# State space stage of a hybrid decoder layer: the instructions of VectorE, ScalarE and TensorE in the order of the kernel's calls

## The chip, the cores and the metric

The kernel runs on one NeuronCore of a Trainium2 chip. The core has five engines that each work through a queue of their own: TensorE (PE in the profile) for matrix products and transposes, VectorE (DVE) and ScalarE (ACT) for element work, GpSimd (POOL) for more element work, and SyncE (SP), which here only issues DMA transfers. An instruction that needs another engine's result waits for a semaphore, and whatever stands behind it on its own engine waits with it. The metric is the device time of one call in microseconds (us), compared by the median of several runs.

## The reference

One layer of a decoder trunk on x of shape (1, 1024, 1024), all in float32. It has three sub-layers: parallel token mixing, cross-attention into 256 memory tokens, and a feed-forward block. The token mixing is a stick-breaking attention beside a Mamba-2 state space mixer (32 heads of 64 in 4 groups, state size 128, chunks of 128 positions), each gated and projected. The part that matters here is the mixer's chunked form. For each group and each chunk of 128 positions:

```
cb     = C . B^T                               (128 x 128, shared by the 8 heads of the group)
decay  = exp(a_cs[l] - a_cs[s]), s <= l        (per head)
y_diag = (cb * decay) . x                      (inside the chunk)
state  = state * exp(a_cs[last]) + B^T . (decay_to_end * x)
y_off  = C . state_before * exp(a_cs)          (from earlier chunks)
y      = (y_diag + y_off + d_skip * x) * silu(z)
y      = y * rsqrt(mean(y*y over the group) + eps) * g_norm
out   += y . w_br_ssm                          (the branch's projection)
```

## The kernel before

**Arithmetic.** Products that need float32 accuracy are made of three passes: each operand is split into a high part (a copy that is rounded, made by ScalarE, `hi_sb`, L119) and a low part (what the rounding lost, made by VectorE, `lo_of`, L122), and `mm3` (L124 to L128) sums high.high, high.low and low.high.

**Stages.** Input projection and convolution come first, then the attention, then the state space stage, then the attention's projection with the gates, the output projection, cross-attention and the feed-forward block. Each stage opens its own pools of buffers and closes them at its end.

**The state space stage** is a software pipeline over 32 steps n (4 groups g of 8 chunks c, `n = 8 g + c`), written as one loop (L1340 to L1361). One pass of the loop calls, in this order:

- `prep(n + 2)`: two matmuls into the banks `dec` (L1137) give the decay's exponents, ScalarE takes the exponentials (L1138), VectorE multiplies them with `cb` (L1139, tile `seg`, 128 x 1024). GpSimd weighs x for the state (L1144, `xw`), and ScalarE and VectorE split it (`s2r`, the high and low part). At each fourth chunk `open_four` loads and splits B and C and makes `cb` (L1114).
- parts of the memory projection for the later cross-attention (`mem_work`), spread over the first eight passes, and for some n the loading and splitting of the branch's weights (`branch_load`, L1236 and L1237).
- one `branch` (12 matmuls into a bank `mm`, and VectorE's addition into the sum `a`, L1250; for group 0 a copy by ScalarE, L1248).
- `states(n + 1)`: three matmuls into `pst`, GpSimd's decay of the state (L1161), VectorE's addition (L1162), then the split of the state into `sth` (ScalarE) and `stl` (VectorE).
- `outp(n)`: GpSimd's d_skip product (L1178), three matmuls into `po`, VectorE's scaling (L1183), GpSimd's addition (L1184), 32 small matmuls into `pd`, VectorE's addition of `pd` (L1194) and product with the gate `zs` (L1195), ScalarE's square with a sum (L1198, tile `junk`), GpSimd's reciprocal root in two instructions (L173 and L174, `rstd`), and ScalarE's scaling of y by it (L1200).
- a second `branch`.
- `flip(n - 2)`: four transposes into the bank `ptr`, whose high part ScalarE takes (L1216, `oth`) and whose low part VectorE takes (L1217, `otl`).

Two `branch` calls stand in each pass from n = 7 on; ten are left over when the loop ends and are called from the next stage, mixed with its loads of the attention's output (`m`, L1408).

**What sets the order.** The kernel is written against a scheduling layer. It takes the calls, simulates a schedule, and puts each engine's instructions into the order of that schedule; an instruction of a later call may so stand ahead of one of an earlier call where no data or buffer forbids it. Three engines are wrapped in a small class, `InTurn` (L34 to L51). While its flag `on` is set, each instruction that is issued through it gets an order edge, on the same engine and without a semaphore, behind the one issued through it before. Before the change the flag is set only around the openings of the cross-attention and feed-forward stages (`in_turn`, L1593, with `opening` and `lead_in`). GpSimd and SyncE are never wrapped.

**Buffers.** In PSUM (eight banks) `dec` and `mm` have two banks each, `pst`, `po`, `pd` and `ptr` one each. In SBUF the pool `t2` gives nine rooms to `xs`, `xw`, `zs`, `y` and `yo` (all shown as `s`), the pool `wr` three to raw weights and to the memory projection's results, and `seg` has three.

Of the kernel before, what the change touches and what calls it, by code (L numbers as in the profile page):

```python
# [54 lines left out]
def hybrid_block(ctx, tc, a, out, dbg=None):  # L55
    nc = tc.nc
    V, A, T = [InTurn(tc, e) for e in (nc.vector, nc.scalar, nc.tensor)]
# [12 lines left out]
    def mk(pl, shape, dt, tag, bufs=None):  # L70
        uid[0] += 1
        kw = {} if bufs is None else {"bufs": bufs}
        return pl.tile(shape, dt, tag=tag, name=f"{tag}_{uid[0]}", **kw)
# [50 lines left out]
    def mm3(ps, sh, sl, mh, ml, start, stop):  # L124
        first = T.matmul(ps, sh, mh, start=start, stop=False)  # L125
        T.matmul(ps, sh, ml, start=False, stop=False)  # L126
        T.matmul(ps, sl, mh, start=False, stop=stop)  # L127
        return first  # L128
# [874 lines left out]
    with ExitStack() as p3:  # L1003
# [112 lines left out]
        def prep(n):  # L1116

            g, c = divmod(n, NCH)
            q, ci = divmod(c, 4)
            if c == 0:  # L1120
                grp[g] = {}
            if ci == 0:
                open_four(g, q)
            f4 = four[g, q]
            cs = slice(ci * P, (ci + 1) * P)
            d = chk[n] = {}
            rows_ = slice(c * P, (c + 1) * P)
            cr = colrows[n % NROW]
            for j in range(2):
                nc.sync.dma_start(cr[ONES + j:ONES + j + 1].bitcast(F32), sum_d[j:j + 1, g * GH:(g + 1) * GH, rows_])  # L1130
            xs = d["xs"] = mk(t2, [P, HALF], F32, "s2")
            nc.sync.dma_start(xs, xs_d[g][rows_, :])
            seg = d["seg"] = mk(t4, [P, GH, P], F32, "s4")
            for j in range(2):
                hs = slice(4 * j, 4 * j + 4)
                pe = mk(ps, [P, 4, P], F32, "dec", bufs=2)
                T.matmul(pe, f4["keys"][:, cs], cr[:, hs, :], start=True, stop=True)  # L1137
                A.activation(seg[:, hs, :], pe, AF.Exp)  # L1138
            V.scalar_tensor_tensor(seg, seg, LARGE, f4["cb"][:, ci, :].unsqueeze(1).to_broadcast([P, GH, P]), ALU.min, ALU.mult)  # L1139
            d["ch"], d["cl"] = f4["ch"][:, cs], f4["cl"][:, cs]  # L1140
            if c < NCH - 1:
                d["bh"], d["bl"] = f4["bh"][:, ci, :], f4["bl"][:, ci, :]
                xw = mk(t2, [P, HALF], F32, "s2")
                G.tensor_tensor(v3(xw), v3(xs), bc(wm, c, g), ALU.mult)  # L1144
                xwh = d["xwh"] = mk(t2, [P, HALF], F32R, "s2r", bufs=4)
                xwl = d["xwl"] = mk(t2, [P, HALF], F32R, "s2r", bufs=4)
                hi_sb(xwh, xw, "a")
                lo_of(xwl, xw, xwh)

        def states(n):  # L1150
            g, c = divmod(n, NCH)
            d, gd = chk[n], grp[g]
            if c == NCH - 1:
                return
            pst_ = mk(ps, [P, HALF], F32, "pst")
            marks.append(mm3(pst_, d["bh"], d["bl"], d["xwh"], d["xwl"], True, True))
            state = mk(gb, [P, HALF], F32, "state")
            if c == 0:
                A.activation(state, pst_, AF.Copy)
            else:  # L1160
                G.tensor_tensor(v3(state), v3(gd["state"]), bc(cdm, c, g), ALU.mult)  # L1161
                V.tensor_tensor(state, state, pst_, ALU.add)  # L1162
            gd["state"] = state
            sth = mk(gb, [P, HALF], F32R, "sth")
            stl = mk(gb, [P, HALF], F32R, "stl")
            hi_sb(sth, state, "a")
            lo_of(stl, state, sth)
            gd["st", c + 1] = (sth, stl)

        def outp(n):  # L1170
            g, c = divmod(n, NCH)
            d, gd = chk[n], grp[g]
            rows_ = slice(c * P, (c + 1) * P)
            seg, xs = d["seg"], d["xs"]
            zs = mk(t2, [P, HALF], F32, "s2")
            nc.sync.dma_start(zs, zs_d[rows_, g * HALF:(g + 1) * HALF])
            y = mk(t2, [P, HALF], F32, "s2")
            G.tensor_tensor(v3(y), v3(xs), dsk[:, g * GH:(g + 1) * GH].unsqueeze(2).to_broadcast([P, GH, HD]), ALU.mult)  # L1178
            if c > 0:
                po = mk(ps, [P, HALF], F32, "po")  # L1180
                mm3(po, d["ch"], d["cl"], *gd["st", c], True, True)
                yo = mk(t2, [P, HALF], F32, "s2")
                V.tensor_tensor(v3(yo), v3(po), bc(eam, c, g), ALU.mult)  # L1183
                G.tensor_tensor(y, y, yo, ALU.add)  # L1184

            pd = mk(ps, [P, HALF], F32, "pd")
            for h in range(GH - 1, -1, -1):
                hs = slice(h * HD, (h + 1) * HD)
                for j in range(2):
                    r = slice(j * HD, (j + 1) * HD)  # L1190
                    ins = T.matmul(pd[r, hs], seg[:, h, r], xs[:, hs], start=True, stop=True)
                    if h == GH - 1 and j == 0:
                        marks.append(ins)
            V.tensor_tensor(y, y, pd, ALU.add)  # L1194
            V.tensor_tensor(y, y, zs, ALU.mult)  # L1195
            junk = mk(jk, [P, HALF], BF16, "junk")
            ms = mk(stats, [P, 1], F32, "ms")
            A.activation(junk, y, AF.Square, scale=float(HALF) ** -0.5, accum_out=ms)  # L1198

            A.activation(y, y, AF.Copy, scale=rstd_of(ms))  # L1200
            d["y"] = y
# [23 lines left out]
        def branch_load(g, fh, kk):  # L1225

            if (g, fh) not in brw:
                brw[g, fh] = halves()
            w = brw[g, fh]
            raw = mk(wr, [P, 2, HALF], F32, "wraw")  # L1230
            r0 = g * HALF + kk * 2 * P
            nc.sync.dma_start(raw, a["w_br_ssm"][0][r0:r0 + 2 * P, fh * HALF:(fh + 1) * HALF].rearrange("(k p) f -> p k f", p=P))
            for j in range(2):
                k = 2 * kk + j
                gain = pcol("g_ssm_norm", g * 4 + k)
                A.activation(w[:, k, 0], raw[:, j], AF.Copy, scale=gain)  # L1236
                V.scalar_tensor_tensor(w[:, k, 1], raw[:, j], gain, w[:, k, 0].bitcast(F32), ALU.mult, ALU.subtract)  # L1237

        def branch(g, half, f):
            oh, ol = grp[g]["oh", half], grp[g]["ol", half]  # L1240
            sl = slice(half * HALF, (half + 1) * HALF)
            w = brw[g, f // 4]
            fs = slice(f % 4 * P, (f % 4 + 1) * P)
            pb = mk(ps, [P, HALF], F32, "mm", bufs=2)
            for k in range(4):
                mm3(pb, w[:, k, 0, fs], w[:, k, 1, fs], oh[:, k, :], ol[:, k, :], k == 0, k == 3)
            if g == 0:
                A.activation(acc[f][:, sl], pb, AF.Copy)  # L1248
            else:
                V.tensor_tensor(acc[f][:, sl], acc[f][:, sl], pb, ALU.add)  # L1250
# [4 lines left out]
        def mem_quanta():  # L1255
# [63 lines left out]
            for i, ps_ in enumerate(parts):  # L1319
                if i + 2 < len(loads):  # L1320
                    yield loads[i + 2]
                yield from ps_

        for n in range(AHEAD):
            prep(n)
        mq = list(mem_quanta())
# [2 lines left out]
        def mem_work(upto):  # L1329
            while mq and NQ - len(mq) < upto:  # L1330
                mq.pop(0)()
# [8 lines left out]
        for n in range(-AHEAD, NN + 2):  # L1340
            if AHEAD <= n + AHEAD < NN:
                prep(n + AHEAD)
            mem_work((n + AHEAD) * NQ / MEM_SPAN)
            for l in loads.pop(n, []):
                branch_load(*l)
            if todo and todo[0][0] <= n:
                todo.pop(0)[1]()
            if 0 <= n + 1 < NN:
                states(n + 1)
            mem_work((n + AHEAD + 0.33) * NQ / MEM_SPAN)  # L1350
            if 0 <= n < NN:
                outp(n)
            mem_work((n + AHEAD + 0.67) * NQ / MEM_SPAN)
            if todo and todo[0][0] <= n:
                todo.pop(0)[1]()
            if 0 <= n - 2 < NN:
                flip(n - 2)
                if (n - 2) % 4 == 3:
                    g, c = divmod(n - 2, NCH)
                    fs = list(range(KT)) if c == 3 else list(range(4, KT)) + list(range(4))  # L1360
                    todo += [(n + 2, lambda g=g, hf_=c // 4, f=f: branch(g, hf_, f)) for f in fs]  # L1361

# [889 lines left out]
```

## Time and profile before

| | |
|---|---|
| runs of the kernel before | 2516.95, 2513.93, 2514.5 us (median 2514.5) |
| the profiled execution | 2516.72 us, of which the span of the trace is 2515.0 us |
| mean granted clock of TensorE | 0.995 |
| PE busy over the span | 2449.4 us (97%), 12306 matmuls |
| DVE busy | 1803.6 us (72%) |
| ACT busy | 1161.5 us (46%) |
| POOL busy | 720.2 us (29%) |
| first and last product with the gate (L1195) in the state space stage | 1105.7 and 1410.4 us |

All of the prediction's times are positions or durations in the profiled execution, in us from the start of its span. A row of the timeline gives start, duration, engine, line, operation, output and inputs, and in brackets how long the engine had been idle and what ended it. "PE" and its weight loads ("PEld") overlap, and neighbouring instructions of one engine overlap by about a tenth of a microsecond, so a sum of durations is a little longer than the time they take. A row with "x32: 671/676/689" gives count, shortest, median and longest duration in ns.

### The profile page before, as it was taken

The page shows a single profiled execution, that of the slowest core. Times are in us where ns is not written, and L with a number is a line of the kernel's source. Part 1 is how long each engine was busy: PE and PEld are TensorE (multiplying, and loading weights), DVE is VectorE, ACT ScalarE, POOL GpSimd, SP SyncE. Part 2 cuts the span into 40 slices and gives each one's busy share as a digit, 9 for nine tenths or more (in the row PEclk, how much of TensorE's full clock was granted, in tenths as well). Part 3 has the DMA queues.
Part 4 walks back from the last instruction along what each step waited for, and adds up shares of the span by engine and source line. Part 5 has one row for each costly group of instructions (what it writes and reads, how often), then busy time and mean ns, then how long its engine had stood idle before and what let it go on. Part 6 is the DMA issues. An engine that isn't in the chain of part 4 may idle for free. (4 is left out here: it accounts for less than half of the span.)

```text
span 2515.0 us, 33312 instructions
## 1 busy us (share of the span) xinstructions
PE 2449.4 (97%) x12306; PEld 2016.7 (80%) x12306; DVE 1803.6 (72%) x2205; ACT 1161.5 (46%) x2054; POOL 720.2 (29%) x581
## 2 busy tenths in 40 slices
PE   7999999999999999999999999999999999999998
PEld 5788888888877888877777787887888888888887
DVE  7665777767587878689888674577368665666997
ACT  5333455555555665566644312344335333344433
POOL 3221545443111111146666241104011332220001
PEclk9999999999999999999999999999999999999999
DMA  7431443333534343366333481322142322234322
GB/s 248 157 118 49 138 145 107 109 101 93 160 97 109 95 117 91 94 191 206 98 100 88 136 273 64 131 94 67 67 151 63 101 80 76 93 98 165 131 101 101
DMA packets 249132, 295.62 MB, mean 118 GB/s; under 512 B 17023, under 2 KB 169096, under 8 KB 248842
## 3 DMA queue, kind: packets, MB, share of 16 engines
q1 hardware_dynamic: 248682, 292.45, 36.9%
q8 instruction: 97, 1.59, 0.3%
q10 hardware_dynamic: 288, 1.05, 0.1%
q14 instruction: 65, 0.53, 0.1%
HBM read 202.20 MB, written 74.45 MB: 110 GB/s over the span
## 5 line engine op out<-in xcount | busy, mean ns | idle before, releaser
L911 DVE TENSOR_TENSOR_SCAN n<-n,mask 128x128 f32<-128x128 f32 (+7 forms) x128 | 189.8, 1510 | 23.7 <-ACT n L910 22.4
L122 DVE TENSOR_TENSOR sw<-sf,sw 128x512 fp32r<-128x512 f32 x142 | 129.5, 916 | 69.6 <-ACT sw L119 67.6
L119 ACT ACTIVATE sw<-sf 128x512 fp32r<-128x512 f32 x142 | 88.9, 628 | 155.8 <-PE mm L230 139.2
L928 ACT ACTIVATE wth<-tr,mone 128x512 fp32r<-128x512 f32 x192 | 110.7, 585 | 83.6 <-PE tr L925 81.7
L929 DVE SCALAR_TENSOR_TENSOR wtl<-tr,wth 128x512 fp32r<-128x512 f32 x192 | 99.7, 544 | 48.6 <-ACT wth L928 48.6
L693 DVE SCALAR_TENSOR_TENSOR b<-b,prmT,b 128x1023 f32<-128x1023 f32 (+2 forms) x72 | 109.7, 1523 | 16.9 <-ACT b L687 16.3
L196 POOL TENSOR_TENSOR sf<-wr,wr 128x512 f32<-128x512 f32 x36 | 51.8, 1438 | 232.7 <-DMA wr<-in_w_gu_dram 95.1
L122 DVE TENSOR_TENSOR sw<-wr,sw 128x512 fp32r<-128x512 f32 x107 | 100.3, 939 | 24.4 <-ACT sw L119 24.3
L229 PE MATMUL mm<-h,sw 128*128 128x512 f32 x288 | 112.0, 389 | 0.0
L230 PE MATMUL mm<-h,sw 128*128 128x512 f32 x288 | 111.7, 389 | 0.0
L228 PE MATMUL mm<-h,sw 128*128 128x512 f32 x288 | 109.9, 389 | 0.0
L910 ACT ACTIVATE n<-sc 128x512 f32<-128x512 f32 (+1 forms) x192 | 88.6, 494 | 45.9 <-PE tr L925 28.7
L173 POOL TENSOR_SCALAR rstd<-ms 128x1 f32<-128x1 f32 x74 | 29.3, 396 | 273.9 <-ACT x L180 195.0
L125 PE MATMUL mm<-oth,bw 128*128 128x512 f32 x256 | 103.7, 405 | 3.1 <-DVE a L1250 3.1
L115 POOL TENSOR_SCALAR v<-va 128x512 fp32r<-128x512 f32 x16 | 20.5, 1282 | 286.3 <-PE av L938 166.3
L127 PE MATMUL p<-bw,h 128*128 128x512 f32 x256 | 100.2, 392 | 0.5 <-DVE h L122 0.5
L127 PE MATMUL mm<-oth,bw 128*128 128x512 f32 x256 | 100.5, 393 | 0.0
L126 PE MATMUL mm<-otl,bw 128*128 128x512 f32 x256 | 100.5, 392 | 0.0
L125 PE MATMUL p<-bw,h 128*128 128x512 f32 x256 | 99.9, 390 | 0.0
L126 PE MATMUL p<-bw,h 128*128 128x512 f32 x256 | 99.8, 390 | 0.0
L925 PE MATMUL tr<-ident,n 128*128 128x128 f32 x576 | 95.5, 275 | 3.6 <-DVE wtl L929 3.6
L119 ACT ACTIVATE zh<-zr 128x512 fp32r<-128x512 f32 x72 | 45.0, 630 | 104.8 <-PE ma L492 52.4
(661 smaller groups left out, 7814.2 us busy)
## 6 DMA issues: line engine op xcount, KB each, us to landing
wr<-in_w_in_dram SPq DMA_DIRECT2D x36, 512.0 KB
wr<-in_w_gu_dram SPq DMA_DIRECT2D x72, 256.0 KB
zr<-in_w_in_dram SPq DMA_DIRECT2D x28, 512.0 KB
wraw<-in_w_in_dram SPq DMA_DIRECT2D x20, 512.0 KB
gu_d<-t SPq DMA_DIRECT2D x36, 256.0 KB
zs_d<-zo SPq DMA_DIRECT2D x32, 256.0 KB
xs_d<-b SPq DMA_DIRECT2D x32, 256.0 KB
kl<-gt SPq DMA_DIRECT2D x64, 128.0 KB
```

What stands on the lines that cost most here:

```text
L119: A.activation(o, i, AF.Copy)
L122: eng.tensor_tensor(o, i, hi.bitcast(F32), ALU.subtract)
L125: first = T.matmul(ps, sh, mh, start=start, stop=False)
L126: T.matmul(ps, sh, ml, start=False, stop=False)
L127: T.matmul(ps, sl, mh, start=False, stop=stop)
L228: T.matmul(ps, w[0][:, k, :], bh, start=first and k == 0, stop=False, skip_group_check=True)
L229: T.matmul(ps, w[0][:, k, :], bl, start=False, stop=False, skip_group_check=True)
L230: ins = T.matmul(ps, w[1][:, k, :], bh, start=False, stop=last and k == 3, skip_group_check=True)
L693: V.scalar_tensor_tensor(acc[:, sh:], y[:, :S - sh], cw(3 - sh, f), acc[:, sh:], ALU.mult, ALU.add)
L911: V.tensor_tensor_scan(nt[:, 0:L][:, ::-1], nt[:, 0:L][:, ::-1], mask[:, S - L:][:, ::-1], 1.0, ALU.mult, ALU.max)
L928: A.activation(wh[:, t0 * P:], pt[:, t0 * P:], AF.Identity, bias=mone)
L929: V.scalar_tensor_tensor(wl[:, t0 * P:], pt[:, t0 * P:], -1.0, wh[:, t0 * P:].bitcast(F32), ALU.add, ALU.subtract)
```

## The change

The flags of all three wrappers are set before the first `prep` call of the state space stage and cleared after its loop:

```diff
@@ -1321,6 +1321,8 @@
                     yield loads[i + 2]
                 yield from ps_
 
+        for e in (V, A, T):
+            e.on = True
         for n in range(AHEAD):
             prep(n)
         mq = list(mem_quanta())
@@ -1359,6 +1361,8 @@
                     g, c = divmod(n - 2, NCH)
                     fs = list(range(KT)) if c == 3 else list(range(4, KT)) + list(range(4))
                     todo += [(n + 2, lambda g=g, hf_=c // 4, f=f: branch(g, hf_, f)) for f in fs]
+        for e in (V, A, T):
+            e.on, e.last = False, None
```

No instruction is added or taken away. Within the stage VectorE, ScalarE and TensorE now stand in the order of the calls listed above. GpSimd's and SyncE's orders come from the schedule as before, which has to follow the three. In the program the wrapped instructions are put down to the wrapper's own line, so in the stage of the changed kernel VectorE, ScalarE and TensorE show as L49.

The pass for n = 27 shows it. ScalarE before the change, from the split of the state on; `junk` is the square of step 27, the two instructions from `dec` are exponentials for step 30, `oth` belongs to step 25's transposes, and the row with `rstd` scales step 27's y:

```order
L119 ACTIVATE sth_13257<-state_13254 128x512
L119 ACTIVATE s2r_13333<-s_2819_13331 128x512
L1198 ACTIVATE junk_13291,ms_13292<-s_2806_13263 128x512
L1216 ACTIVATE oth_13209<-ptr_13312 128x4x128
L1138 ACTIVATE s_2816_13323<-dec_13324 128x512
L1138 ACTIVATE s_2816_13323<-dec_13327 128x512
L1200 ACTIVATE s_2806_13263<-s_2806_13263,rstd_13294 128x512
```

The same instructions on ScalarE after the change:

```order
L49 ACTIVATE sth_13257<-state_13254 128x512
L49 ACTIVATE junk_13291,ms_13292<-s_2806_13263 128x512
L49 ACTIVATE s_2806_13263<-s_2806_13263,rstd_13294 128x512
L49 ACTIVATE oth_13209<-ptr_13312 128x4x128
L49 ACTIVATE s_2816_13323<-dec_13324 128x512
L49 ACTIVATE s_2816_13323<-dec_13327 128x512
L49 ACTIVATE s2r_13333<-s_2819_13331 128x512
```

The scaling of y has moved from behind the copy out of `ptr` and the two exponentials to a place in front of all three, right behind the square that its `rstd` is made from.

VectorE in the same pass before the change; `s_2794` is `seg` of step 29, the two `a` rows are the two branches, `s_2808` is the scaled `po`, and the rows with `s_2806` are the addition of `pd` and the product with the gate:

```order
L122 TENSOR_TENSOR s2r_13233<-s_2797_13230,s2r_13232 128x512
L1217 TENSOR_TENSOR otl_13210<-ptr_13211,oth_13209 128x4x128
L1139 SCALAR_TENSOR_TENSOR s_2794_13222<-s_2794_13222,cb_13113 128x1024
L1250 TENSOR_TENSOR a_2049_9939<-a_2049_9939,mm_13236 128x512
L1162 TENSOR_TENSOR state_13254<-state_13254,pst_13250 128x512
L1183 TENSOR_TENSOR s_2808_13269<-po_13265,eam_2335 128x512
L122 TENSOR_TENSOR stl_13258<-state_13254,sth_13257 128x512
L1194 TENSOR_TENSOR s_2806_13263<-s_2806_13263,pd_13272 128x512
L1195 TENSOR_TENSOR s_2806_13263<-s_2806_13263,s_2805_13261 128x512
L1250 TENSOR_TENSOR a_2049_9939<-a_2049_9939,mm_13298 128x512
```

And after the change:

```order
L49 TENSOR_TENSOR otl_13210<-ptr_13211,oth_13209 128x4x128
L49 SCALAR_TENSOR_TENSOR s_2794_13222<-s_2794_13222,cb_13113 128x1024
L49 TENSOR_TENSOR s2r_13233<-s_2797_13230,s2r_13232 128x512
L49 TENSOR_TENSOR a_2049_9939<-a_2049_9939,mm_13236 128x512
L49 TENSOR_TENSOR state_13254<-state_13254,pst_13250 128x512
L49 TENSOR_TENSOR stl_13258<-state_13254,sth_13257 128x512
L49 TENSOR_TENSOR s_2808_13269<-po_13265,eam_2335 128x512
L49 TENSOR_TENSOR s_2806_13263<-s_2806_13263,pd_13272 128x512
L49 TENSOR_TENSOR s_2806_13263<-s_2806_13263,s_2805_13261 128x512
L49 TENSOR_TENSOR a_2049_9939<-a_2049_9939,mm_13298 128x512
```

The split of x (`s2r`) now stands behind `seg`, and the low part of the state (`stl`) in front of the scaling of `po` that GpSimd's addition waits for.

## Prediction

> **What bounds the kernel now.** I read the busy time by stretches first, then one pass of the loop engine by engine, then the spread of single operations, and last the places that anchor the sum. Steps 0 to 5 of the state space stage lie between 1086 and 1176 us, steps 6 to 31 between 1176 and 1410; the columns are PE, PEld, DVE, ACT and POOL busy, then the granted clock, DMA share and GB/s:
>
> ```profile
> 1086.00:1176.00 90.00, 82.66 (x630) 68.44 (x629) 80.38 (x83) 56.67 (x99) 51.36 (x41) 0.96 0.65 202
> 1176.00:1410.00 234.00, 228.06 (x1711) 183.59 (x1710) 200.20 (x258) 125.14 (x243) 139.26 (x134) 1.00 0.36 107
> ```
>
> PE is busy 97% of the longer stretch and VectorE 86%: two engines near their limit, neither waiting long for the other. A pass is next seen on each engine. ScalarE, then VectorE, then GpSimd, around step 27:
>
> ```profile
> 1377.68 0.63 ACT L1198 ACTIVATE junk<-s 128x512 bf16<-128x512 f32 x1
> 1378.22 0.19 ACT L1198 ACTIVATION_READ_ACCUMULATOR junk<-s 128x1 f32 x1
> 1378.31 0.58 ACT L1216 ACTIVATE oth<-ptr 128x512 fp32r<-128x512 f32 x1
> 1378.79 1.08 ACT L1138 ACTIVATE s<-dec 128x512 f32<-128x512 f32 x2
> 1380.08 0.72 ACT L1200 ACTIVATE s<-s,rstd 128x512 f32<-128x512 f32 x1 [0.21 <-POOL rstd L174]
> ```
>
> ```profile
> 1370.87 1.21 DVE L1139 SCALAR_TENSOR_TENSOR s<-s,cb 128x1024 f32<-128x1024 f32 x1
> 1372.01 0.67 DVE L1250 TENSOR_TENSOR a<-a,mm 128x512 f32<-128x512 f32 x1
> 1372.60 0.68 DVE L1162 TENSOR_TENSOR state<-state,pst 128x512 f32<-128x512 f32 x1
> 1373.20 0.68 DVE L1183 TENSOR_TENSOR s<-po,eam 128x512 f32<-128x512 f32 x1
> 1374.04 0.91 DVE L122 TENSOR_TENSOR stl<-state,sth 128x512 fp32r<-128x512 f32 x1 [0.16 <-ACT sth L119]
> 1376.13 0.69 DVE L1194 TENSOR_TENSOR s<-s,pd 128x512 f32<-128x512 f32 x1 [1.18 <-POOL s L1184]
> 1376.85 0.80 DVE L1195 TENSOR_TENSOR s<-s,s 128x512 f32<-128x512 f32 x1
> 1377.57 0.68 DVE L1250 TENSOR_TENSOR a<-a,mm 128x512 f32<-128x512 f32 x1
> 1378.17 1.15 DVE L122 TENSOR_TENSOR s2r<-s,s2r 128x512 fp32r<-128x512 f32 x1
> 1379.24 0.68 DVE L1217 TENSOR_TENSOR otl<-ptr,oth 128x512 fp32r<-128x512 f32 x1
> 1379.90 1.22 DVE L1139 SCALAR_TENSOR_TENSOR s<-s,cb 128x1024 f32<-128x1024 f32 x1
> ```
>
> ```profile
> 1374.36 1.74 POOL L1184 TENSOR_TENSOR s<-s,s 128x512 f32<-128x512 f32 x1
> 1376.06 1.04 POOL L1144 TENSOR_TENSOR s<-s,wm 128x512 f32<-128x512 f32 x1
> 1377.72 1.04 POOL L1178 TENSOR_TENSOR s<-s,dsk 128x512 f32<-128x512 f32 x1 [0.63 <-DVE s L1195]
> 1378.85 0.54 POOL L173 TENSOR_SCALAR rstd<-ms 128x1 f32<-128x1 f32 x1
> 1379.48 0.57 POOL L174 TENSOR_TENSOR rstd<-rstd,mhalf 128x1 f32<-128x1 f32 x1
> ```
>
> VectorE's two `seg` products (L1139) lie 9.03 us apart: that is a pass. The reader should see how little waits: VectorE 1.18 us for GpSimd's addition and 0.16 for the state's high part, ScalarE 0.21 us for the reciprocal root. That last wait is short because the copy from `ptr` and two exponentials run between the square and the scaling, while GpSimd makes the root. The exponentials for a later `seg` thus do not wait for the current step's y.
>
> **What the new order joins.** ScalarE now has to finish square, root and scaling before `oth` and the exponentials; VectorE meets `seg` before anything else of the pass, and the product with the gate near its end. So each pass closes a ring over three engines: exponentials, `seg`, `s2r`, branch addition, state addition, `sth`, `stl`, scaled `po`, GpSimd's addition, addition of `pd`, gate product, square, root, scaling, `oth`, exponentials of the next pass. PE is not in the ring. It is gated by freed banks only (`dec` by the exponentials, `pd` by its addition, `mm` by the branch additions), and its results of a pass can be ready a good part of a pass early.
>
> The ring, step by step. Two durations are taken from operations that nothing disturbs, since GpSimd has little to do in the first half of the ring; count, shortest, median, longest in ns:
>
> ```profile
> L1184 POOL TENSOR_TENSOR s<-s,s x28: 1282/1726/3401, 1111.4 to 1407.9; 128x512 f32<-128x512 f32 x28
> ...
> L122 DVE TENSOR_TENSOR s2r<-s,s2r x28: 676/854/1523, 1090.6 to 1378.2; 128x512 fp32r<-128x512 f32 x28
> ```
>
> - exponentials 1.08 and hand-over 0.03; `seg` to the next start (1372.01 - 1370.87) 1.14: together 2.25.
> - `s2r` undisturbed 0.68, of which 0.60 to the next start, as VectorE's rows 1372.60 and 1373.20 stand apart; branch addition 0.60; state addition 0.68: 4.13.
> - from the end of the state addition (1373.28) to `stl` (1374.04), which holds ScalarE's `sth`: 0.76; `stl` undisturbed 0.60; scaled `po` 0.68: 6.17.
> - GpSimd's addition 1.28 at its shortest, since `stl` now is over when it starts, and 0.05 to hand over: 7.50.
> - end of GpSimd's addition (1376.10) to end of the gate product (1377.65): 1.55, so 9.05; from there to the root's end (1380.05): 2.40, so 11.45. Here L1178 stood between; where it gets its room earlier, the root starts right behind the accumulator's row (1378.41) and needs 0.08 + 0.63 + 0.57, which is 0.36 less.
> - scaling 0.03 + 0.62 to the next start, `oth` 0.48 (1378.79 - 1378.31): 12.58, or 12.2 without L1178 in between.
>
> I take **12.4 us a pass** against 9.03 seen here. VectorE's second branch addition and `otl` lie beside the square and the exponentials and cost nothing. With the median 1.73 for GpSimd's addition a pass would take 13.0.
>
> **What differs from the plain pass.** Groups of the stage (busy us, mean ns, idle before):
>
> ```profile
> L122 DVE TENSOR_TENSOR bw<-wraw,bw 128x1024 fp32r<-128x1024 f32 x16 | 24.8, 1557 | 5.2 <-ACT bw L119 5.1
> L1237 DVE SCALAR_TENSOR_TENSOR bw<-wraw,prmT,bw 128x512 fp32r<-128x512 f32 x32 | 23.5, 781 | 2.0 <-ACT bw L1236 1.6
> ...
> L119 ACT ACTIVATE bw<-wraw 128x1024 fp32r<-128x1024 f32 x16 | 16.9, 1059 | 12.0 <-DMA wraw<-in_w_xkv_dram 12.0
> ...
> L122 DVE TENSOR_TENSOR cl<-cfm,ch 128x512 fp32r<-128x512 f32 x7 | 7.1, 1009 | 0.0
> ```
>
> From n = 6 to 30 (25 passes): 13 branch loads put two L1237 into the ring, 1.35 each time (2 x 0.78 less overlaps): +17.5. Six openings of a new four put the splits of B and C and `cb` ahead of `seg`, some 2.6 us beside exponentials of 1.1, so 1.5 each: +9. Four passes have no state (-2.05 each), three no `s2r` (-0.6), three no `po` (-2.0), the last no exponentials, `seg` and `s2r` (-2.8); a rest of memory work adds 1.5. Sum +9, so 25 x 12.4 + 9 = 319 us.
>
> Passes 0 to 5 hold the memory projection: two raw weights each, one whose high and low part (1.06, 1.13 to 1.56) both stand in the ring, one whose high part does and whose low part runs partly beside the exponentials. That is 2.0 to 2.2 and 1.3 to 1.6, while the branch addition (0.6) is missing: 15.2 a pass; pass 0 lacks `po` and `oth`, 11.3.
>
> **The sum.** Anchors of before: five raw weights stand ahead of the first pass in the new order, and the fifth is split at
>
> ```profile
> 1107.72 1.06 ACT L119 ACTIVATE bw<-wraw 128x1024 fp32r<-128x1024 f32 x1
> ```
>
> held by its transfer, so pass 0 starts at about 1109. The `pd` additions of steps 0, 31 and 6 and the last transposes:
>
> ```profile
> L1194 DVE TENSOR_TENSOR s<-s,pd x32: 671/676/689, 1104.5 to 1409.2; 128x512 f32<-128x512 f32 x32
> ...
> 1175.73 0.67 DVE L1194 TENSOR_TENSOR s<-s,pd 128x512 f32<-128x512 f32 x1
> ...
> L1213 PE MATMUL ptr<-ident,s x128: 270/272/329, 1126.4 to 1421.4; 128*128 128x128 f32 x128
> ```
>
> 1. Up to step 6: pass 6 starts at 1109 + 11.3 + 5 x 15.2 = 1196, its addition 7.7 us into the pass at 1204, against 1175.7: +28.
> 2. Steps 6 to 31: pass 31 starts 319 us later at 1515, its addition 4.0 us in (no exponentials): 1519, which is 315.3 against 233.5: +82.
> 3. The tail: two more passes of two branches each with `flip` are PE's own work, transposes at about 1530 against 1421: -1 against step 31's lead. Ten branches are left over in both kernels, with the same loads of `m`: 0.
>
> Together +109. Against the profiled execution, 2516.7 + 109 = 2626; the median of the runs shown lies 2.2 us lower, so **2624 us**. GpSimd's and SyncE's queues cost nothing here: their loads are due a pass ahead. If that cover goes, a late transfer now stops the whole ring: the group above shows 12.0 us of ScalarE's waits for raw weights already, hidden so far; these 12 would come on top, 20 if they grow with it.
>
> The likeliest case's own range is 2595 to 2675: below, a ring of 12.2 and fewer disturbances (-5), openings and loads hidden behind ScalarE's queue (-20); above, 13.0 a pass (+15), waits for raw weights (+20), and late branches (+15).
>
> **A rule against it.** PE would be idle 3.4 us of 12.4. Where it idled before, the clock fell (same columns as above):
>
> ```profile
> 1162.50:1164.20 1.70, 0.00 (x0) 0.00 (x0) 1.70 (x3) 1.70 (x3) 0.00 (x0) 1.00 0.81 242
> 1164.20:1167.40 3.20, 3.19 (x8) 2.52 (x9) 3.20 (x4) 2.31 (x5) 1.88 (x2) 0.50 0.12 40
> ```
>
> After 1.7 us without matmuls the granted clock is 0.50 for 3.2 us. PE's 9.03 us of work a pass at half clock would be 18.1, and PE would be the ring: (18.1 - 12.4) x 25 = +142 more. One such stretch costs 1.6 us, two a pass still leave 12.3, and an engine busy without a break has no idle to lose its clock by. So I leave it out of the sum. The Trainium skill ("TensorE: Matmul & The Clock Gate", "A second HAM failure mode: psum-queue depth-cycling") says that many small pauses between groups of matmuls make the clock swing between half and full; by it the sum would lie between mine and 2764, and I take my rows.
>
> **The rivals.**
> - *PE at half clock becomes the ring*, as above: 2680 to 2764. For it, the rows; against it, that full work restores the clock. 10%.
> - *The ring is not closed*: if ScalarE's scaling does not hold back the exponentials, VectorE's own work sets the pass. Its row above, 9.03 less the wait of 1.18 plus 0.76 for `sth`, gives 8.6 to 9.5 us a pass, 2515 to 2545. For it, that the next `dec` is ready early; against it, the place of the scaling. 8%.
> - *Faster*: the call order serves PE better. PE is idle 5.9 us of the 234, and 7.3 of the 90; if no matmul ever waited, it would gain 13: 2501. It decides only if a pass stays below 9.03. 5%.
> - *No change that shows* (within 0.2%, about 5 us, which is what a measurement of this kernel can tell): 3%, only if the two orders had the same waits.
>
> My forecast has 74%. The range 2580 to 2685 holds it, the lower part of the half-clock case, and leaves out most of the rest. Slower by over 0.2% is 92%, within it 3%, faster 5%.
>
> **What would show it.** Right: `pd` additions about 12.4 us apart from step 9 on; ScalarE idle some 2 us ahead of each scaling, ended by the root; VectorE idle ahead of `seg` for the exponentials and ahead of the `pd` addition for GpSimd; PE busy about 75%; last transposes of the stage near 1530. Wrong: PE busy throughout at a low clock, ScalarE waiting mostly for raw weights, or passes near 9 us.

## The result and the profile after

| | before | after |
|---|---|---|
| median, us | 2514.8 (2513.93 to 2516.95) | 2661.19 (2659.28 to 2663.75) |
| profiled execution, us | 2516.72 | 2662.06, span 2660.3 |
| mean granted clock of TensorE | 0.995 | 0.973 |
| addition of `pd` of step 0, of step 6, of step 31 | 1104.48, 1175.73, 1409.22 | 1120.02, 1224.07, 1552.65 |

The changed kernel takes 1.0578 times the time of before, with an interval of 1.0563 to 1.0592. Of the 145.3 us between the two profiled executions, 48.3 have arisen at the addition of step 6 (1224.07 - 1175.73), 95.1 between steps 6 and 31 (328.6 against 233.5), and 1.9 behind it.

Busy time by stretches of after, from the addition of step 0 to that of step 6, and on to that of step 31 (columns as in the prediction: PE, PEld, DVE, ACT, POOL, granted clock, DMA share, GB/s):

```profile
1120.02:1224.07 104.05, 65.38 (x453) 53.10 (x453) 51.21 (x64) 40.39 (x71) 27.77 (x31) 0.82 0.40 130
1224.07:1552.65 328.58, 248.95 (x1704) 195.90 (x1705) 186.03 (x253) 125.42 (x242) 120.75 (x135) 0.88 0.25 76
```

PE was busy 97% of the longer stretch and now is 76%, VectorE 57%; no engine is near its limit. What sets the pass is seen in a plain one. ScalarE of after, around step 11:

```profile
1282.46 0.63 ACT L49 ACTIVATE junk<-s 128x512 bf16<-128x512 f32 x1 [4.50 <-DVE s L49]
1283.00 0.19 ACT L49 ACTIVATION_READ_ACCUMULATOR junk<-s 128x1 f32 x1
1284.32 0.72 ACT L49 ACTIVATE s<-s,rstd 128x512 f32<-128x512 f32 x1 [1.14 <-POOL rstd L174]
1284.95 0.58 ACT L49 ACTIVATE a<-mm 128x512 f32<-128x512 f32 x1
1285.43 0.58 ACT L49 ACTIVATE oth<-ptr 128x512 fp32r<-128x512 f32 x1
1285.91 1.08 ACT L49 ACTIVATE s<-dec 128x512 f32<-128x512 f32 x2
```

VectorE of after, from the exponentials' `seg` on:

```profile
1287.02 1.23 DVE L49 SCALAR_TENSOR_TENSOR s<-s,cb 128x1024 f32<-128x1024 f32 x1 [0.28 <-ACT s L49]
1288.17 0.69 DVE L49 TENSOR_TENSOR s2r<-s,s2r 128x512 fp32r<-128x512 f32 x1
1288.77 0.68 DVE L49 TENSOR_TENSOR state<-state,pst 128x512 f32<-128x512 f32 x1
1290.21 0.91 DVE L49 TENSOR_TENSOR stl<-state,sth 128x512 fp32r<-128x512 f32 x1 [0.76 <-ACT sth L49]
1291.04 0.68 DVE L49 TENSOR_TENSOR s<-po,eam 128x512 f32<-128x512 f32 x1
1293.13 0.69 DVE L49 TENSOR_TENSOR s<-s,pd 128x512 f32<-128x512 f32 x1 [1.41 <-POOL s L1184]
1293.85 0.79 DVE L49 TENSOR_TENSOR s<-s,s 128x512 f32<-128x512 f32 x1
1298.27 0.69 DVE L49 TENSOR_TENSOR otl<-ptr,oth 128x512 fp32r<-128x512 f32 x1 [3.62 <-ACT oth L49]
1299.24 1.23 DVE L49 SCALAR_TENSOR_TENSOR s<-s,cb 128x1024 f32<-128x1024 f32 x1 [0.28 <-ACT s L49]
```

GpSimd of after, in the same pass:

```profile
1291.80 1.30 POOL L1184 TENSOR_TENSOR s<-s,s 128x512 f32<-128x512 f32 x1 [1.23 <-DVE s L49]
...
1295.63 0.22 POOL L173 TENSOR_SCALAR rstd<-ms 128x1 f32<-128x1 f32 x1
1295.94 0.57 POOL L174 TENSOR_TENSOR rstd<-rstd,mhalf 128x1 f32<-128x1 f32 x1
```

Read in order of time, each row starts where another engine's ends: exponentials, `seg`, `s2r`, state, `sth`, `stl`, `po`, GpSimd's addition, `pd`, gate, square, root, scaling, copies, exponentials. From `seg` to `seg` it is 12.22 us, where it was 9.03. (In group 0 the branch's sum is a copy by ScalarE, `a<-mm`, and no addition by VectorE.)

Every fourth pass is longer: it opens a new four. TensorE of after, in the opening of pass 10:

```profile
1258.31 1.06 PE L49 MATMUL dec<-cfm,bfm 128*128 128x128 f32 x8
1259.12 0.48 PE L49 MATMUL dec<-colrows,keyrows 128*128 128x512 f32 x1
1270.10 0.79 PE L49 MATMUL dec<-colrows,keyrows 128*128 128x512 f32 x1 [10.49 <-ACT s L49]
1270.69 0.63 PE L49 MATMUL mm<-oth,bw 128*128 128x512 f32 x1
...
1275.65 0.62 PE L49 MATMUL pst<-s2r,bh 128*128 128x512 f32 x2
```

VectorE of after, in the same place:

```profile
1272.70 0.69 DVE L49 TENSOR_TENSOR s2r<-s,s2r 128x512 fp32r<-128x512 f32 x1
1276.55 0.69 DVE L49 TENSOR_TENSOR state<-state,pst 128x512 f32<-128x512 f32 x1 [3.16 <-PE pst L49]
```

An opening puts three products into the two banks of `dec`: `cb` (here from `cfm` and `bfm`) and the two halves of the exponents. The third can start only when the first half's bank is free, that is, behind this pass's own first exponential (ScalarE ends it at 1270.04; VectorE reads `cb` only from 1270.36 on), and PE, in order, stands still for 10.49 us. Its lead of most of a pass is gone, it returns at half clock (granted 0.50 over the next 5.3 us), and VectorE's addition of the state waits for it. The pass takes 18.39 us from addition to addition.

### The profile page after: what moved, and what is told of

Read it like the earlier page. It is cut to its first block, busy times and chain, and to the rows that moved or that the text cites. A ratio compares the mean times of both kernels' runs of the same rounds, so it can differ in the third digit from the quotient of the medians.

```text
span 2660.3 us, 33306 instructions
## 1 busy us (share of the span) xinstructions
PE 2474.4 (93%) x12306; PEld 2033.3 (76%) x12306; DVE 1783.7 (67%) x2205; ACT 1162.9 (44%) x2054; POOL 690.4 (26%) x581
## 5 line engine op out<-in xcount | busy, mean ns | idle before, releaser
L49 PE MATMUL mm<-oth,bw 128*128 128x512 f32 x432 | 160.9, 436 | 26.8 <-DVE a L49 17.4
L49 PEld LDWEIGHTS mm<-oth,bw 128*128 128x128 f32 x432 | 90.7, 210 | 53.7 <-DVE a L49 18.0
L49 PE MATMUL dec<-colrows,keyrows 128*128 128x512 f32 x64 | 27.9, 497 | 73.5 <-ACT s L49 73.5
L115 POOL TENSOR_SCALAR v<-va 128x512 fp32r<-128x512 f32 x16 | 20.6, 1287 | 285.1 <-PE av L938 166.0
L49 PE MATMUL mm<-otl,bw 128*128 128x512 f32 x216 | 92.3, 427 | 0.0
L119 ACT ACTIVATE sw<-wr 128x512 fp32r<-128x512 f32 x107 | 67.1, 628 | 57.0 <-PE mm L230 51.8
```

The lines of the kernel that those rows point to most:

```text
L49: self.last = call(*args, **kw)
L119: A.activation(o, i, AF.Copy)
```

## The experiments

The table puts the runs together. "6 to 31" is the time between the additions of `pd` of these steps in each profiled execution, "pass 11" the time from the addition of step 10 to that of step 11, "pass 10" the same for the opening before it, "pass 5" for the pass of the memory projection that is slowest in after. The ratio is against the kernel before, in runs on the same chip, where its median was 2514.8 to 2516.9; a difference to after, in microseconds, compares medians from different sets of runs and is good to about 2 us. No kernel leaves work out.

| run | median, us | ratio, interval | 6 to 31 | pass 5 | pass 10 | pass 11 |
|---|---|---|---|---|---|---|
| before | 2514.8 | | 233.5 | 9.5 | 11.0 | 9.4 |
| after | 2661.2 | 1.0563 to 1.0592 | 328.6 | 23.0 | 18.4 | 12.2 |
| scale_late | 2608.4 | 1.0351 to 1.0389 | 282.0 | 22.5 | 15.2 | 10.3 |
| square_late | 2571.6 | 1.0196 to 1.0236 | 258.8 | 15.1 | 10.4 | 9.0 |
| act_free | 2545.6 | 1.0102 to 1.0132 | 247.7 | 15.8 | 10.4 | 9.1 |
| act_only | 2534.6 | 1.0059 to 1.0093 | 252.7 | 12.6 | 10.5 | 12.4 |
| pe_only | 2536.7 | 1.0063 to 1.0100 | 249.6 | 11.7 | 13.3 | 9.3 |
| dve_only | 2546.8 | 1.0105 to 1.0143 | 247.2 | 15.4 | 11.2 | 9.1 |
| pst_four_times | 2670.1 | 1.0589 to 1.0621 | 332.6 | 26.0 | 18.6 | 12.2 |
| before_pst_four_times | 2563.9 | 1.0167 to 1.0198 | 268.8 | 15.2 | 10.6 | 9.4 |
| pm_bank | 2639.5 | 1.0477 to 1.0508 | 314.2 | 23.4 | 14.0 | 12.4 |
| before_pm_bank | 2514.0 | 0.9982 to 1.0002 | 237.4 | 9.5 | 9.5 | 10.8 |
| both_open | 2563.2 | 1.0166 to 1.0207 | 257.6 | 15.1 | 10.4 | 10.2 |
| own_rooms | 2654.4 | 1.0525 to 1.0560 | 325.8 | 24.4 | 17.0 | 12.2 |

### Is it the ring?

**scale_late.** The call order stays, but the root and the scaling are called one pass later, so on ScalarE the exponentials no longer stand behind it:

```diff
-            A.activation(y, y, AF.Copy, scale=rstd_of(ms))
-            d["y"] = y
+            d["y"], d["ms"] = y, ms
+
+        def scaling(n):
+            y = chk[n]["y"]
+            A.activation(y, y, AF.Copy, scale=rstd_of(chk[n]["ms"]))
...
                 prep(n + AHEAD)
+            if 0 <= n - 1 < NN:
+                scaling(n - 1)
```

> Call order on all three engines, but the reciprocal root and the scaling of step n are called one pass later, behind prep. Ring theory: root and scaling leave the ring, the square and oth stay: 9.05 + 0.65 + 0.5 and hand-overs = 10.3 us a plain pass, 2 us less, so 25 x 2 = 50 us less from step 6 on and up to 12 before: 2598 to 2615 us. Rival (TensorE's dec banks and half clock): the openings stay as they are and the total stays above 2640 us.

Measured: 2608.4 us, 53 less than after, and plain passes of 10.3 to 11.0 (one of 11.5). VectorE's additions of `pd` of this kernel in two neighbouring plain passes:

```profile
1266.29 0.69 DVE L49 TENSOR_TENSOR s<-s,pd 128x512 f32<-128x512 f32 x1 [1.41 <-POOL s L1184]
...
1276.63 0.69 DVE L49 TENSOR_TENSOR s<-s,pd 128x512 f32<-128x512 f32 x1 [1.39 <-POOL s L1184]
```

They are 10.34 us apart, as the ring without root and scaling gives. Steps 6 to 31 lost 46.6 us of their 95.1. Its ScalarE shows why: the exponentials follow the square and two copies at once, and the scaling behind them waits for nothing.

```profile
1278.18 0.63 ACT L49 ACTIVATE junk<-s 128x512 bf16<-128x512 f32 x1 [4.49 <-DVE s L49]
1278.72 0.19 ACT L49 ACTIVATION_READ_ACCUMULATOR junk<-s 128x1 f32 x1
1278.81 0.58 ACT L49 ACTIVATE a<-mm 128x512 f32<-128x512 f32 x1
1279.29 0.59 ACT L49 ACTIVATE oth<-ptr 128x512 fp32r<-128x512 f32 x1
1279.76 1.09 ACT L49 ACTIVATE s<-dec 128x512 f32<-128x512 f32 x2
1280.72 0.65 ACT L49 ACTIVATE s2r<-s 128x512 fp32r<-128x512 f32 x1
1281.24 0.74 ACT L49 ACTIVATE s<-s,rstd 128x512 f32<-128x512 f32 x1
```

**square_late.** The square goes the same way:

```diff
+            d["y"] = y
+
+        def scaling(n):
+            y = chk[n]["y"]
             junk = mk(jk, [P, HALF], BF16, "junk")
             ms = mk(stats, [P, 1], F32, "ms")
             A.activation(junk, y, AF.Square, scale=float(HALF) ** -0.5, accum_out=ms)
-
             A.activation(y, y, AF.Copy, scale=rstd_of(ms))
-            d["y"] = y
...
                 prep(n + AHEAD)
+            if 0 <= n - 1 < NN:
+                scaling(n - 1)
```

> Call order on all three engines, but square, root and scaling of step n are called one pass later, behind prep and its exponentials. Ring theory: the ring is open, ScalarE's exponentials wait for nothing of the same pass but the copy oth; what is left is VectorE's own row of a pass with its waits for sth and GpSimd's addition, 9.2 to 9.8 us a plain pass, 2.6 to 3.1 us less than in full call order, so 65 to 78 us less from step 6 on and some 15 before: 2565 to 2590 us. Rival (TensorE in call order needs about 10.5 us a pass with its waits and half clock): no faster than with the scaling alone moved, 2600 us or more.

Measured: 2571.6 us, 89.6 less than after, with every engine still in the order of the calls. VectorE of this kernel:

```profile
1243.33 0.69 DVE L49 TENSOR_TENSOR s<-s,pd 128x512 f32<-128x512 f32 x1 [1.40 <-POOL s L1184]
...
1249.65 0.69 DVE L49 TENSOR_TENSOR stl<-state,sth 128x512 fp32r<-128x512 f32 x1 [1.62 <-ACT sth L49]
1250.26 0.68 DVE L49 TENSOR_TENSOR s<-po,eam 128x512 f32<-128x512 f32 x1
1252.35 0.69 DVE L49 TENSOR_TENSOR s<-s,pd 128x512 f32<-128x512 f32 x1 [1.40 <-POOL s L1184]
...
1266.87 1.41 DVE L49 SCALAR_TENSOR_TENSOR bw<-wraw,prmT,bw 128x512 fp32r<-128x512 f32 x2 [2.13 <-ACT bw L49]
```

Passes 11 and 12 take 9.02 us, as short as before: in them VectorE waits only for `sth` and for GpSimd's addition, and the 3.62 us ahead of `otl` are gone. Not every pass is so short. The mean of the 25 is 10.4 us (258.8 / 25; 9.3 in before), and other plain passes reach 11.6, above the 9.2 to 9.8 that were expected. Most of these hold a branch load, as the last row shows: ScalarE's part of it now stands behind the scaling, which waits for the root, and VectorE waits for ScalarE, 20.6 us in 11 places of steps 6 to 31. The wait has thus moved in part and is not gone. The place of two instructions on ScalarE, with their root, carries 61% of the loss (89.6 of 146.4 us).

**act_free**, **act_only**, **pe_only**, **dve_only.** The flag is set for some of the engines only:

```diff
-        for e in (V, A, T):
+        for e in (V, T):
             e.on = True
```

and `(A,)`, `(T,)`, `(V,)` in the other three.

> VectorE and TensorE in call order, ScalarE left to the schedule, which puts a step's square and scaling behind the next exponentials. Ring theory (the ring over ScalarE, VectorE and GpSimd sets the pass, and ScalarE's place for square and scaling closes it): plain passes of 9.0 to 9.8 us between additions of pd, whole kernel 2525 to 2575 us. Rival (TensorE's order costs the time: a third use of the two dec banks at each opening of a four, and the half clock behind it): the openings keep their extra 6 us each and the passes stay near 12 us, 2620 us or more.

> ScalarE alone in call order, VectorE and TensorE left to the schedule. Ring theory: the ring needs VectorE's order too (seg ahead of the rest of a pass); without it the addition of pd of a step waits only for exponentials made three passes earlier, so passes of 9.0 to 9.8 us, whole kernel 2515 to 2560 us. Rival (ScalarE's own order is enough, since the exponentials stand behind a scaling that waits 2 us for the root): passes of 11 us or more, 2590 us or more.

> TensorE alone in call order, VectorE and ScalarE left to the schedule. Ring theory: no ring, since neither seg nor the exponentials are held behind the y of the same pass; 2512 to 2540 us. Rival (TensorE's order is what costs: dec banks and half clock): 2580 us or more. The prediction's rival of a gain (the call order serves TensorE better): about 2501 us.

> VectorE alone in call order, ScalarE and TensorE left to the schedule. Ring theory: ScalarE's free place for the scaling leaves the ring open, VectorE's own row with its waits sets the pass at 9.2 to 10 us: 2520 to 2550 us. If seg's place on VectorE alone closes a ring, 2590 us or more.

Measured: 2545.6, 2534.6, 2536.7 and 2546.8 us; all four in the ranges that the ring theory gave for the whole kernel, and none in those of its rivals. The passes fit less well: those of act_only and act_free are 10.1 and 9.9 us on average (252.7 / 25 and 247.7 / 25) where 9.0 to 9.8 was expected, and single passes of act_only swing between 6.7 and 13.1, so that its pass 11 of 12.4, taken alone, would speak for the rival; the mean and the total speak against it. ScalarE's order alone costs 19 us, and VectorE's and TensorE's together 30, no more than VectorE's alone (31); all three in one kernel cost 146. Some 97 us thus arise only where ScalarE's order meets that of the others, which is what a ring over several engines is. TensorE's order by itself gains nothing, so the rival of a gain by it (2501) falls. Not tried was ScalarE's order with that of VectorE alone or of TensorE alone, so whether two engines close the ring is read from the rows and not from a run; and what the 19 to 31 us of a single engine are was not followed up.

### Is TensorE at half clock the bound?

**pst_four_times** and **before_pst_four_times.** The same edit in after and in before, which issues each state product four times over:

```diff
-            marks.append(mm3(pst_, d["bh"], d["bl"], d["xwh"], d["xwl"], True, True))
+            marks.append([mm3(pst_, d["bh"], d["bl"], d["xwh"], d["xwl"], True, True) for _ in range(4)][0])
```

> Call order on all three engines, and the three matmuls of each state product (pst) are issued four times over, which gives the same result and adds 9 matmuls of 0.23 us, 2.1 us of TensorE's work to each of 28 passes (58 us). Ring theory: TensorE has 2 to 3 us of room in a plain pass, so plain passes stay at 12.2 to 12.8 us and the granted clock in the stage rises; openings, where TensorE is late, lose up to 2 each: 2655 to 2690 us. Rival (TensorE at half clock is the bound): each pass is longer by 2.1 to 4.2 us, 2720 to 2777 us.

> The kernel before with the same 252 added matmuls. TensorE is busy 97% of the stage there, so nearly all of the 58 us should show: 2560 to 2580 us. If it shows much less, TensorE is not what bounds the kernel before, and the comparison with the same edit in call order says little.

Measured: after becomes 8.9 us longer, before 46.9 of the 58 (2563.9 against 2516.9 in the same set of runs). Steps 6 to 31 of after with the added work:

```profile
1229.72:1562.32 332.60, 281.00 (x1893) 225.03 (x1892) 188.13 (x254) 125.56 (x242) 121.78 (x135) 0.93 0.25 76
```

PE is busy 281 us and no longer 249, and the stretch grew by 4.0 us only; most plain passes are 12.2 to 12.7 (three 13.3 to 13.5), and the granted clock rises from 0.88 to 0.93. The same stretch of before with the added work:

```profile
1184.73:1453.50 268.77, 268.75 (x1898) 217.96 (x1897) 208.67 (x258) 126.80 (x245) 138.92 (x135) 1.00 0.32 94
```

Here PE is busy without a break and the stretch grew by 35.3. TensorE bounded the stage before and does not after. Since the added matmuls also raise the clock, they might in part have paid for themselves, and the run alone does not exclude that; the waits of after do not fit it. Of VectorE's waits in steps 6 to 31, 9.2 us are ended by TensorE, 101.2 by ScalarE and 31.4 by GpSimd. The half clock is there, but is not the ring.

### What does an opening cost?

**pm_bank.** The product `cb` goes through the bank `pst`, which the pass before has left:

```diff
-            pm = mk(ps, [P, 4, P], F32, "dec", bufs=2)
+            pm = mk(ps, [P, 4, P], F32, "pst")
```

> Call order on all three engines, but the product cb of an opening goes through the bank pst and no longer through dec. Plain passes stay at 12.2 to 12.4 us in every theory. If an opening's extra 6 us come from the third use of two dec banks (TensorE waits for the pass's own first exponential and loses its lead), the seven openings shrink by 4 to 5 us each: 2626 to 2635 us, and TensorE's waits of 8 to 12 us at its second dec product of an opening are gone. Rival (the splits of B and C on ScalarE and VectorE are what an opening costs): 2650 us or more.

Measured: 2639.5 us, 21.7 less, where 26 to 35 were expected: below the rival's 2650, and above the range of the theory. The opening of pass 10 on VectorE:

```profile
1254.69 0.69 DVE L49 TENSOR_TENSOR s<-s,pd 128x512 f32<-128x512 f32 x1 [1.40 <-POOL s L1184]
1268.69 0.69 DVE L49 TENSOR_TENSOR s<-s,pd 128x512 f32<-128x512 f32 x1 [1.40 <-POOL s L1184]
```

14.00 us, 4.4 less than after. Passes 18 and 26 went from 18.23 and 15.92 to 13.95 and 13.94 (pass 14, which has no state product, grew by 1.0), and steps 6 to 31 take 314.2. But TensorE has a new wait, in the same pass:

```profile
1251.08 1.16 PE L49 MATMUL pst<-cfm,bfm 128*128 128x128 f32 x8 [0.45 <-DVE state L49]
1252.00 0.71 PE L49 MATMUL dec<-colrows,keyrows 128*128 128x512 f32 x2
...
1262.37 1.22 PE L49 MATMUL pst<-s2r,bh 128*128 128x512 f32 x2 [6.91 <-DVE cb L49]
```

The state product now waits 6.91 us for VectorE to read `cb` out of the bank. Both exponents are made ahead of that, so less is late, and a part of the expected gain stays behind.

**before_pm_bank** and **both_open.** The same edit in the kernel before, and in square_late:

> The kernel before with the product cb of an opening in the bank pst. TensorE waits 6.5 us for the dec banks in the whole stage there, so at most 6 us are to be had, and the new wait of pst for the addition of cb can take them back: 2508 to 2520 us.

> Call order on all three engines with both edits: square, root and scaling called a pass later, and the product cb of an opening in the bank pst. If the two losses are apart, the bank still takes away TensorE's 17 us of waits at dec that are left with the square late, of which some 10 to 15 lie on the path: 2556 to 2564 us. If the ring was the only reason that an opening's third use of dec hurt, 2567 to 2575 us.

Measured: 2514.0 us (ratio 0.9982 to 1.0002), no change that can be told; and 2563.2 against 2571.6. The second is undecided: the medians lie in the range of "two losses apart", but the profiled executions (spans of 2566.3 and 2564.6) and steps 6 to 31 (257.6 and 258.8) hardly differ, and square_late's runs spread over 11 us. No run was faster than the kernel before beyond its interval.

### Why is pass 5 so long?

**own_rooms.** The memory projection's results leave the three rooms of raw weights:

```diff
-                        o = mk(wr, [P, D], F32, "wraw")[:, :ML]
+                        o = mk(t2, [P, HALF], F32, "s2")[:, :ML]
...
-                        o = mk(wr, [P, D], F32, "wraw")[:, :HALF]
+                        o = mk(t2, [P, HALF], F32, "s2")
```

> Call order on all three engines, but the memory projection's results go through the nine rooms of pool t2, so that the three rooms of pool wr hold raw weights alone. If the raw weights of passes 4 to 6 come late because their rooms are held by results, the 23 us between the additions of steps 4 and 5 fall to 15 to 17, ScalarE's waits for raw weights (10.4 + 3.6 us up to step 6) shrink to under 5, and the kernel takes 2645 to 2654 us. Rival (SyncE's queue issues them late, being held by loads that wait for TensorE's dec products): nothing changes, 2657 to 2665 us.

Measured: 2654.4 us, at the upper end of the range. ScalarE's waits for raw weights up to step 6, 14.0 us in after, are gone, and yet pass 5 takes 24.4. The gain of 6.8 does come in part from these waits, but at another place: step 0's addition lies 4.2 us earlier. In after a late raw weight stands right in front of that addition, first on ScalarE and then on VectorE:

```profile
1117.79 1.06 ACT L49 ACTIVATE bw<-wraw 128x1024 fp32r<-128x1024 f32 x1 [3.38 <-DMA wraw<-in_w_xkv_dram]
1118.88 1.23 DVE L49 TENSOR_TENSOR bw<-wraw,bw 128x1024 fp32r<-128x1024 f32 x1 [3.67 <-ACT bw L49]
```

In pass 5 there is a longer wait. On TensorE of after it is

```profile
1186.80 1.22 PE L49 MATMUL mm<-bw,mh 128*128 128x512 f32 x2 [8.02 <-ACT wraw L49]
```

on TensorE of own_rooms

```profile
1183.56 1.22 PE L49 MATMUL mm<-bw,mh 128*128 128x512 f32 x2 [8.50 <-ACT s L49]
```

and on its ScalarE:

```profile
1182.93 1.06 ACT L49 ACTIVATE s<-mm 128x512 f32<-128x512 f32 x2
...
1194.88 1.34 ACT L49 ACTIVATE bw<-wraw,prmT 128x512 fp32r<-128x512 f32 x2 [8.47 <-PE mm L49]
```

TensorE's memory products wait for ScalarE's copies out of `mm`, which stand behind square and scaling; and the splitting of the branch's weights then waits for TensorE, by the row's releaser for the last memory products out of the room `bw` that it writes to. So in pass 5 the raw weights were late beside a longer wait. The table agrees with that: pass 5 stays at 22.5 with the scaling moved, and falls to 15.1 with the square moved too, and to 15.8 with ScalarE free.

## Why the prediction was right, and where it was short

The measured time lies in the range, but 37 us above the forecast of 2624. The openings and pass 5, which make up most of that, stood neither in the sum at their size nor among what widened the range, so that the range was wide enough for them is luck; that the ring is what costs is not.

- **The ring, 12.4 us a pass.** Right. Plain passes are 12.2 to 12.6 (12.0 to 12.1 in passes 9, 17 and 25), and the rows stand one behind another as listed; GpSimd's addition takes the 1.28 to 1.30 us that were taken for it. The lower value of 12.2 holds where L1178 does not stand between gate and root: ScalarE's wait ahead of the scaling is then 1.14 us and not 2. scale_late and square_late took the ring apart and got 10.3 and 9.0 in their shortest plain passes.
- **"Six openings ... so 1.5 each."** This term of step 2 failed (five of the six lie between the additions of steps 6 and 31). Passes 10, 18 and 26 take 18.4, 18.2 and 15.9, which is 3.5 to 6 more than a plain pass. The sentence behind it that fails is "PE is not in the ring ... its results of a pass can be ready a good part of a pass early": with three products for two banks of `dec`, PE waits for the pass's own first exponential and has no lead. With `cb` in another bank the openings of passes 10, 18 and 26 take 13.9 to 14.0, which is 1.5 above a plain pass, and steps 6 to 31 take 314.2 against the forecast 315.3; with `dec` they took 328.6. The other terms of step 2 thus hold in sum, but not one by one: passes 13, 21 and 29, with a branch load and without `s2r`, come to 13.15 by its terms (12.4 + 1.35 - 0.6) and took 12.4 to 12.6, while passes 16 and 24, with a branch load and without `po`, come to 11.75 and took 12.3. That these errors cancel is luck.
- **Passes 0 to 5, 15.2 each, and step 6's addition at 1204.** 20 us short. The openings of passes 2 and 6 account for 8.2 (pm_bank has 95.8 us between the additions of steps 0 and 6, after 104.05). Pass 5 is 7.8 longer than 15.2, since copies out of `mm` stand behind the square; the sum had no term for them. That leaves some 4 us. The anchor held (the fifth raw weight is split at 1107.97), but the next one was 3.38 us late ahead of step 0's addition, which is most of them.
- **"GpSimd's and SyncE's queues cost nothing here."** Raw weights did come late, 14.0 us of waits up to step 6, near the 12 to 20 given for it. Put at nothing, this term was wrong by some 3 to 4 us, ahead of step 0's addition; in pass 5 the waits lay beside a longer one. own_rooms took all of them away and gained 6.8.
- **The tail, -1.** It measured +1.9. The last transposes of the stage are at 1565.7 and not near 1530, as the sum of the above.
- **PE's half clock, left out.** Rightly as a bound, by pst_four_times and the waits of after. (Its upper end is 2624 + 142 = 2766, and not 2764.) The clock does swing, with a mean of 0.88 over steps 6 to 31, and PE is busy 249 us for the same work that took 228. The section of the Trainium skill cited there ("TensorE: Matmul & The Clock Gate", "A second HAM failure mode: psum-queue depth-cycling") says the same of a kernel whose pauses between groups of matmuls are small and frequent. In steps 6 to 31 of after the pauses that were followed by half clock were of 2.0 us or more.
- **The rivals.** A ring that is not closed, a gain, and no change fall with the result; the first two would have needed ScalarE's free place for square and scaling (act_free, square_late) or a gain from TensorE's order (pe_only, +21).

## What to carry to other kernels

When engines are put into program order, write down for each the first instruction of a pass and what it stands behind on its own engine, and follow these across the engines until the line meets itself: where that ring is longer than any engine's own work, its length is the pass, however idle each engine is. Then count the uses of each rotating buffer in the irregular passes as well as in the plain ones; one use more than there are buffers tied TensorE, which ran ahead, to the present pass here. An instruction with a long wait ahead of it (a norm's square and scaling) belongs behind whatever the next pass needs from the same engine, and calling it a pass later gave back 61% of the loss here with the three engines still in call order. What then stands behind it on the same engine waits in its turn, as the branch loads of square_late did.

## What the runs showed of the hardware that was not expected

The clock's fall does not follow from the length of a pause alone. Four stretches of after, columns as above; PE is idle in the first, all but the first 1.4 us of the third, and the second and fourth follow them:

```profile
1240.20:1243.80 3.60, 0.04 (x2) 0.00 (x0) 0.00 (x0) 1.24 (x3) 3.17 (x5) 1.00 0.18 68
1243.80:1247.00 3.20, 3.18 (x9) 2.56 (x10) 2.43 (x3) 3.20 (x7) 0.00 (x0) 0.64 0.00 0
1306.00:1309.90 3.90, 1.15 (x32) 1.01 (x32) 0.90 (x2) 1.94 (x5) 0.79 (x2) 0.96 0.08 25
1309.94:1313.05 3.11, 3.11 (x7) 2.50 (x8) 2.36 (x3) 3.11 (x6) 0.00 (x0) 0.51 0.00 0
```

A pause of 3.6 us left the clock at 1.00 until work had begun again, and it then fell in the midst of the work (0.64 over 3.2 us); one of 2.5 us had halved it at the first matmul, as had the one of 1.7 us in the prediction's rows. In steps 6 to 31 of after no pause of up to 1.4 us lowered the clock (one of 0.5 us at 1233 met a clock that a pause of 2.0 had just halved). Of the six of 2.0 to 3.7 us four were followed by a slow first matmul, those of 2.7 and 3.6 were not, and each of the five of 9 us or more was. The pause of 10.5 us:

```profile
1259.60:1270.10 10.50, 0.01 (x2) 0.00 (x1) 4.44 (x7) 3.94 (x8) 4.96 (x6) 0.60 0.22 75
1270.10:1275.40 5.30, 5.30 (x13) 4.14 (x14) 2.77 (x4) 1.12 (x2) 0.00 (x0) 0.50 0.46 143
```

It was followed by 5.3 us at 0.50, against 3.2 in the prediction's rows. And more work made the clock faster: 252 added matmuls raised the mean of steps 6 to 31 from 0.88 to 0.93.
